# Aligning the programs of VectorE and ScalarE to blocks of 128 instructions in a fused LoRA matmul

## The chip, the cores and the metric

The kernel runs on one core of a Trainium2 chip. The metric is the device time of one execution in microseconds (us), the median of several runs. Before the change it is 161.82 us (three runs, 161.81 to 161.85).

## What is computed

A linear layer with a low-rank addition. `x` has 16 x 2048 = 32,768 rows of 256 numbers; the weights are 256 x 256, the rank is 16, and everything outside the kernel is float32.

```python
x_flat = x.reshape(-1, in_dim)
y = x_flat @ W
lora_out = x_flat @ lora_A
lora_out = lora_out * lora_E
lora_out = lora_out @ lora_B
y = y + scale * lora_out
return y.reshape(batch, seq_len, out_dim).astype(np.float32)
```

Some 33.6 MB have to be read and as many written.

## The kernel before

The kernel first folds the low-rank part into one matrix, `weff` = W + A diag(E) B, in bf16 (lines 159 to 177). After that the whole work is `x_flat @ weff`.

The rows are cut into five blocks of 56, 56, 48, 48 and 48 times 128 rows (`PLAN`). Three SBUF slots (`xy0` to `xy2`) hold a block each; x is loaded into a slot, the result is written over it in place, and the slot is stored from there. Block 3 uses slot 0 again and block 4 slot 1, so load 3 has to wait for store 0 and load 4 for store 1. Loads 0 to 3 are cut into pieces of 16 or 24 rows per partition (`PIECES`), each with its own semaphore; load 4 and all stores are single transfers. All of these are issued by SP (SyncE) in the order that the code writes out: loads 0 to 2, store 0, store 1, load 3, load 4, stores 2 to 4. Some have an extra wait: store 1 is issued after TensorE's 17th group of transposes, load 4 after the 19th, store 3 after the 28th (`ISSUE_STORE`, `ISSUE_LOAD`). lora_A, lora_B and lora_E are loaded from ScalarE's queue.

The computing goes in 32 steps of 8 x 128 rows. Per step `t`:

- VectorE casts 8 rows per partition to bf16 into `xb` (`rounded`, line 152), after a wait for the piece's load where a piece begins.
- TensorE transposes them into `psum_xt` (line 191), and VectorE copies that to `xt` (`copied`, line 156).
- TensorE multiplies with `weff` into `psum_y`, two halves of 4 x 128 rows (line 202).
- ScalarE copies each half back into the slot as float32 (line 225).

VectorE's order is `copied(t)`, `rounded(t + 2)`. VectorE's and ScalarE's programs are written out in full, all 32 steps; TensorE's is a loop of 16 rounds over two steps (line 212). At step 17 VectorE pauses (`HOLD = 17, 1`): it executes ten no-operations (lines 149 and 150) and then waits until store 1 has landed (line 151) before it casts step 17. All engines after VectorE pause with it.

The transfers written between lines 124 and 130 are issued before the meeting of all engines at line 132; the rest comes behind it. At the end VectorE, ScalarE, TensorE and SP count the semaphores back to zero (lines 245 to 253).

[...]

Of the kernel before, what the change touches and what calls it, by code (L numbers as in the profile page):

```python
# [35 lines left out]
def kernel(tc, x, W, lora_A, lora_B, lora_E, scale, out):  # L36
    nc = tc.nc
# [60 lines left out]
    def slot(i):  # L98
        return slots[i % LEAD][:, :PLAN[i], :]
# [20 lines left out]
        nc.tensor.wait_ge(sem, 1).then_inc(sem, -1)  # L120

    opening.append(tc.info.no_tile_sem_insts)
    transfer(nc.sync, s_w, out=w_sb, in_=W.rearrange("(p c) m -> p c m", c=KC))
# [17 lines left out]
    def rounded(t):  # L143
        i, r = steps[t]
        if (i, r) in s_ld:
            nc.vector.wait_ge(s_ld[i, r].sem, 16)
        if t == HOLD[0]:

            for _ in range(10):
                nc.vector.engine_nop()  # L150
            nc.vector.wait_ge(s_st[HOLD[1]].sem, 16)
        nc.vector.tensor_copy(out=xb[t % 2], in_=slot(i)[:, r:r + S, :]).then_inc(can_t[t % 2], 1)  # L152

# [22 lines left out]
    nc.vector.wait_ge(s_set.sem, 2)  # L176
    s_v.by(nc.vector.tensor_add(out=weff, in0=w_sb, in1=ps_aeb))  # L177
    rounded(0)
    rounded(1)
    for t in range(NS):  # L180
        copied(t)
        if t + 2 < NS:
            rounded(t + 2)
# [105 lines left out]
```

## Time and profile before

| what | value |
|---|---|
| median of three runs | 161.82 us (161.81 to 161.85) |
| the profiled execution's own time | 161.88 us |
| its span, first to last instruction | 160.6 us |
| moved by the DMA engines | 67.42 MB, mean 420 GB/s |
| busy: TensorE, VectorE, ScalarE | 93.9, 76.5, 63.2 us |
| granted TensorE clock, mean | 0.832 |

The span is shorter than the time by 1.3 us, which lies around it. Busy shares of the computing engines are between 39% and 58%, since they work in three stretches, with the pause from 55 to 87 us and the drain of the last stores, from 140 us, between and behind them. "DMA" in the chain of waits is time in which an instruction waited for a transfer to land. A bracket at the end of a timeline line gives the engine's idle time before that instruction and what ended it. In the list of DMA queues the columns are packets, MB, and the time that the packets took as a share of the span of all 16 DMA engines; asked for a window, the view counts the packets that start in it, so a share over 100% means only that they end outside it.

Beside the views, the trace holds every DMA packet with its start, duration and size, and every landing, 16 for each transfer (one of each DMA engine).

### The profile page before, as it was taken

The page shows a single profiled execution, that of the slowest core. Times are in us where ns is not written, and L with a number is a line of the kernel's source. Part 1 is how long each engine was busy: PE and PEld are TensorE (multiplying, and loading weights), DVE is VectorE, ACT ScalarE, POOL GpSimd, SP SyncE. Part 2 cuts the span into 40 slices and gives each one's busy share as a digit, 9 for nine tenths or more (in the row PEclk, how much of TensorE's full clock was granted, in tenths as well). Part 3 has the DMA queues.
Part 4 walks back from the last instruction along what each step waited for, and adds up shares of the span by engine and source line. Part 5 has one row for each costly group of instructions (what it writes and reads, how often), then busy time and mean ns, then how long its engine had stood idle before and what let it go on. Part 6 is the DMA issues. An engine that isn't in the chain of part 4 may idle for free.

```text
span 160.6 us, 1871 instructions
## 1 busy us (share of the span) xinstructions
PE 93.9 (58%) x780; PEld 84.2 (52%) x780; DVE 76.5 (48%) x67; ACT 63.2 (39%) x65; POOL 0.7 (0%) x6
## 2 busy tenths in 40 slices
PE   0159979999999920000000899999569999700000
PEld 0039959999999910000000789999458999500000
DVE  0178679998989300000002968987094985000000
ACT  1101746867777640000000077777605586800000
POOL 1000000000000000000000000000000000000000
PEclk9999999999999997555555599999955999995555
DMA  5999999999999999999998999999999999999994
GB/s 158 426 433 451 435 408 433 449 441 404 459 410 392 457 459 457 457 457 443 443 414 347 404 453 429 435 529 404 404 392 478 465 429 392 416 478 441 416 404 196
DMA packets 2658, 67.42 MB, mean 420 GB/s; under 512 B 464, under 2 KB 480, under 8 KB 608
## 3 DMA queue, kind: packets, MB, share of 16 engines
q1 hardware_dynamic: 2448, 67.37, 97.7%
q10 hardware_dynamic: 208, 0.03, 0.3%
q14 instruction: 2, 0.02, 0.0%
HBM read 33.85 MB, written 33.55 MB: 420 GB/s over the span
## 4 chain that ended last, share of the span: by engine, by line
PE 36%; DMA 34%; DVE 2%; ACT 1%; issue 0%; SPq 0%
PE psum_y L202 23%; DMA out_dram<-xy 20%; DMA xy<-in_x_dram 14%; PE psum_xt L191 13%; DVE xb L152 2%; ACT xy L225 1%; SPq L241 0%; SPq L236 0%
## 5 line engine op out<-in xcount | busy, mean ns | idle before, releaser
L225 ACT COPY xy<-psum_y 128x1024 f32<-128x1024 f32 x64 | 61.9, 1017 | 73.7 <-PE psum_y L202 73.7
L202 PE MATMUL psum_y<-weff,xt 128*128 128x256 bf16 x512 | 64.4, 281 | 0.1
L191 PE MATMUL psum_xt<-ident,xb 128*128 128x128 f32 x264 | 38.1, 293 | 37.9 <-DVE xb L152 37.9
L152 DVE CAST xb<-xy 128x2048 bf16<-128x2048 f32 x32 | 38.9, 1219 | 41.4 <-DMA out_dram<-xy 33.5
L202 PEld LDWEIGHTS psum_y<-weff,xt 128*128 128x128 bf16 x512 | 51.8, 101 | 7.4 <-issue 0.3
L191 PEld LDWEIGHTS psum_xt<-ident,xb 128*128 128x128 f32 x264 | 33.1, 152 | 39.6 <-DVE xb L152 39.2
L156 DVE COPY xt<-psum_xt 128x1024 f32<-128x1024 f32 x32 | 39.1, 1222 | 10.4 <-PE psum_xt L191 10.3
L164 PE MATMUL psum_xt<-ident,a_sb 128*16 128x128 f32 x2 | 0.6, 394 | 4.2 <-POOL ident L138 4.2
L160 DVE CAST b_bf<-b_sb 16x256 bf16<-16x256 f32 x1 | 0.3, 280 | 5.4 <-DMA b_sb<-in_lora_B_dram 5.4
L225 ACT ACT_TABLE_LOAD x1 | 1.3, 1283 | 3.5 <-PEq L132 3.5
L173 PE MATMUL psum_xt<-b_bf,ate 16*128 16x256 bf16 x2 | 0.6, 403 | 3.2 <-DVE ate L168 3.2
L164 PEld LDWEIGHTS psum_xt<-ident,a_sb 128*16 128x16 f32 x2 | 0.1, 90 | 4.2 <-DMA a_sb<-in_lora_A_dram 4.2
L173 PEld LDWEIGHTS psum_xt<-b_bf,ate 16*128 16x128 bf16 x2 | 0.1, 105 | 3.7 <-DVE ate L168 3.7
L168 DVE TENSOR_SCALAR ate<-psum_xt,e_sb 16x256 bf16<-16x256 f32 x1 | 0.5, 471 | 1.8 <-DMA e_sb<-in_lora_E_dram 1.8
L177 DVE TENSOR_TENSOR weff<-w_sb,psum_xt 128x512 bf16<-128x512 f32 x1 | 0.7, 689 | 0.8 <-PE psum_xt L173 0.8
L138 POOL TENSOR_SCALAR_AFFINE_SELECT ident<-ident 128x128 f32<-128x128 f32 x1 | 0.3, 293 | 0.2 <-POOL ident L136 0.2
L136 POOL MEMSET ident<- 128x128 f32 x1 | 0.2, 205 | 2.9 <-POOLq L132 2.9
L270 POOL MEMSET const-bfloat16-1.0<- 128x1 bf16 x1 | 0.1, 102 | 0.0
L270 POOL MEMSET const-uint8-127<- 128x1 uint8 x1 | 0.1, 102 | 0.0
L270 POOL MEMSET const-float32-0.0<- 128x1 f32 x1 | 0.1, 99 | 0.2 <-issue 0.2
L270 POOL MEMSET const-float32-1.0<- 128x1 f32 x1 | 0.1, 99 | 0.0
## 6 DMA issues: line engine op xcount, KB each, us to landing
xy<-in_x_dram SPq DMA_DIRECT2D x6, 3072.0 KB, 32.5
out_dram<-xy SPq DMA_DIRECT2D x3, 6144.0 KB, 21.5
out_dram<-xy SPq DMA_DIRECT2D x2, 7168.0 KB, 33.9
xy<-in_x_dram SPq DMA_DIRECT2D x4, 2048.0 KB, 17.6
xy<-in_x_dram SPq DMA_DIRECT2D x1, 6144.0 KB, 21.9
w_sb<-in_W_dram SPq DMA_DIRECT2D x1, 256.0 KB, 2.8
a_sb<-in_lora_A_dram ACTq DMA_DIRECT2D x1, 16.0 KB, 3.0
b_sb<-in_lora_B_dram ACTq DMA_DIRECT2D x1, 16.0 KB, 4.2
```

Source lines behind the costliest of these rows:

```text
L138: s_id.by(nc.gpsimd.affine_select(out=ident, in_=ident, compare_op=mybir.AluOpType.not_equal, fill=1.0, base=0, pattern=[[-1, P]], channel ...
L152: nc.vector.tensor_copy(out=xb[t % 2], in_=slot(i)[:, r:r + S, :]).then_inc(can_t[t % 2], 1)
L156: nc.vector.tensor_copy(out=xt[t % 2], in_=ps_xt[t % 2]).then_inc(can_m, 1)
L160: s_v.by(nc.vector.tensor_copy(out=b_bf, in_=b_sb))
L164: at_done = nc.tensor.transpose(ps_at[:, c, :], a_sb[:, c, :], ident)
L168: s_v.by(nc.vector.tensor_scalar(out=ate, in0=ps_at, scalar1=e_sb, scalar2=float(scale), op0=mybir.AluOpType.mult, op1=mybir.AluOpType.mult))
L173: aeb_done = nc.tensor.matmul(ps_aeb[:, c, :], ate[:, c, :], b_bf, start=True, stop=True)
L177: s_v.by(nc.vector.tensor_add(out=weff, in0=w_sb, in1=ps_aeb))
L191: done = nc.tensor.transpose(ps_xt[k][:, j, :], words[k][:, j, :], ident)
L202: done = nc.tensor.matmul(ps_y[h][:, j, :], pairs[k][:, h * G + j, :, c], weff[:, c, :], start=(c == 0), stop=(c == KC - 1))
L225: y = nc.scalar.copy(out=slot(i)[:, r:r + G, :], in_=ps_y[h])
L270: nc = _bacc.Bacc("TRN2", target_bir_lowering=False, num_devices=1)
```

## The change

Ahead of the first transfer, VectorE's and ScalarE's programs get an alignment directive. [...] The ten no-operations ahead of VectorE's wait in the pause are taken out. SP's, TensorE's and GpSimd's programs, every transfer, every wait and the order of all other instructions stay.

```diff
     def take(sem):
         nc.tensor.wait_ge(sem, 1).then_inc(sem, -1)
 
+
+    for engine in (nc.vector, nc.scalar):
+        engine.addr_align(128, offset=0, max_nops=0)
 
 
     opening.append(tc.info.no_tile_sem_insts)
@@ -145,9 +148,6 @@
         if t == HOLD[0]:
-
-            for _ in range(10):
-                nc.vector.engine_nop()
             nc.vector.wait_ge(s_st[HOLD[1]].sem, 16)
```

## The prediction

> **What bounds the kernel now.** I read the page first: the row of DMA busy tenths, the queues and the chain of waits; then the merged chain in order of time, the waits, the timeline around the places where VectorE waits, the DMA view of two short windows, and last the trace's single DMA packets.
>
> ```profile
> span 160.6 us, 1871 instructions
> DMA  5999999999999999999998999999999999999994
> q1 hardware_dynamic: 2448, 67.37, 97.7%
> q14 instruction: 2, 0.02, 0.0%
> ```
>
> The 16 DMA engines are busy in nearly every slice; the data queue alone fills 97.7% of their time. The last row is the code: two packets in the span, 0.02 MB together.
>
> ```profile
> 55.47 31.98 DMA out_dram<-xy
> ...
> 94.65 21.92 DMA xy<-in_x_dram
> ...
> 139.39 1.02 ACT xy L225
> ```
>
> ```profile
> DVE xb L152 <- DMA out_dram<-xy: 33.5, 1, 33.5
> DVE xb L152 <- DMA xy<-in_x_dram: 7.7, 2, 5.0
> ```
>
> ```profile
> 21.27 1.23 DVE L152 CAST xb<-xy 128x2048 bf16<-128x2048 f32 x1 [2.67 <-DMA xy<-in_x_dram]
> ```
>
> The computing engines wait for transfers: 2.67 us at the third piece of block 0, 33.46 us in the pause until store 1 has landed, 5.04 us for load 4. The chain's instructions end at 140.4 us; the remaining 20.2 us is the last store draining. The data queue takes transfers in order, and each is issued while others still run: store 1 at 55.47, while the data packets of store 0 run until about 69.1 to 70.0; load 4 at 94.65, with load 3 running until 100.6 to 101.6; store 3 at 124.55, store 2 running until 129.6 to 130.6; store 4 at 140.43, store 3 running until 144.1 to 145.6. No issue comes late, so the end is set by the work of the slowest DMA engine.
>
> That I take from the packet records. I sorted the data packets by start and strung each to the one that had just ended; 16 strings come out, one per DMA engine, each with 128 large packets of x and y, eight per 128-row transfer. A store packet of 57,344 bytes takes 2116 ns in the median, one of 49,152 bytes 1815. Thirteen engines put their last byte out at 158.61 to 159.20 us, and three later:
>
> - engine S at 159.47: it carried a code packet of 8,192 bytes at 108.02 (309 ns), and the data packet behind it took 2195 ns, 380 too many. Together 0.69.
> - engine V at 159.63: a code packet at 58.74 (309 ns), and 2474 ns for the next, 358 too many. Together 0.67.
> - engine Z at 160.06: no code packet. Its packets from 115.4 to 141.9, the stores during which TensorE and ScalarE compute, take 16 to 137 ns too long, about 1.10 us in all; during store 1, in the pause, they don't.
>
> Z's last landing, 160.54, ends the span.
>
> ```profile
> q1 hardware_dynamic: 80, 4.59, 106.1%
> q14 instruction: 1, 0.01, 0.2%
> issues: line engine op xcount, KB each, median us to landing
> out_dram<-xy SPq DMA_DIRECT2D x1, 7168.0 KB, 32.0
> ```
>
> That is the DMA view from 54 to 64 us: one code packet in the store phase. A second falls in the window from 104 to 112.
>
> **The change part by part.** *The ten no-operations* are recorded from 53.94 to 54.07 us: 0.13 us, inside the 33.46 us that VectorE waits anyway. Gain 0; without the pause 0.13.
>
> *Where the code packets go.* VectorE's no-operations run 4.7 us ahead of the packet at 58.74; ScalarE's copies at 102.7 to 103.3, about as many instructions into its program, run about 5 us ahead of the one at 108.02. I take these for the two engines that are aligned. That is inferred: the packets bear no engine's name. [...] After the alignment point VectorE has 99 instructions in the trace, 89 without the no-operations, and ScalarE 79; both fit in 128. [...]
>
> *What they cost there.* Before 1.75 us no data packet runs, and 15 of the engines have a gap of 0.10 to 0.96 us around 4 us between their first large packets (V 0.35, S 0.27). The trace doesn't show a code packet in the opening. Bounds: 0, if it falls into a gap, and 0.69 as in the middle. I take 0.3, nearer to the opening with its gaps. V then ends at 159.63 - 0.67 + 0.3 = 159.26 (158.96 to 159.65), S at 159.47 - 0.69 + 0.3 = 159.08 (158.78 to 159.47). Both stay ahead of Z even at the upper bound.
>
> *Z.* It carries neither packet. Its surplus goes with the computing during stores 2 and 3, which lasts as long as before: 24 us for 1.10 us, 0.05 per us. Z stays at 160.06, and with it the end.
>
> *What else moves.* V brings store 1's last landing (87.45; the next is 87.17) and load 4's (116.57; S 116.42, the next 116.15). Without these VectorE resumes 0.28 and 0.42 us earlier, and the last store is issued 0.42 earlier, behind 3.7 to 5.2 us of store 3. Gain 0; with that cover gone, up to 0.42. Shifting the computing by 0.42 us under Z's stores is 0.02.
>
> *The entry itself.* [...] Bounds: 0, and some 5 us as from the no-operations to the end of the code packet (54.0 to 59.05). ScalarE has the issues of lora_A, lora_B and lora_E behind it (0.74, 1.17, 1.65 us), and the meeting of all engines at L132, behind which SP issues the next five loads. SP's queue would not run dry: load 0 lands until 21.25 us. The set-up and the first steps would be late, up to 2.67 us of it swallowed at the third piece, the rest at the pause, since store 1 would go out at 58 instead of 55.5 and store 0 runs until 69.1. If that cover were gone, it would be one for one. I take 0.
>
> The sum: 0 for the no-operations, 0 for the packets on V and S as Z ends later, 0 at the entry, -0.02 to +0.02 on Z. The profiled execution took 161.88 (span 160.6 and 1.3 around it), its runs 161.82 in the median; the sum of 0 carries over, **161.8**.
>
> [...]
>
> **The rivals.**
>
> *Z is not there in the timed runs.* If Z's surplus comes from recording the computing (records written while stores are written), the timed runs end with V, and lose 159.63 less the slowest ordinary engine, 159.20 or V with its opening packet, 159.26: 0.37 to 0.43. That gives 161.4. For it: the surplus sits on one engine and only while instructions run during stores. Against it: the profiled execution took 161.88, only 0.06 above the median, where 0.4 would be expected.
>
> [...]
>
> *It does not do what it says.* The two packets belong to other engines, or a crossing remains late in the programs: V and S stay as they are, Z still ends, 161.8, not to be told from the forecast.
>
> **How the numbers follow.** A difference under 0.2%, 0.32 us, is about what a measurement of this kernel can't tell from no change. No change by Z, with the case that nothing moves: 0.43. Z absent, or smaller once V and S are out of its way: 0.35, at 161.4. Dearer front: 0.22, at 162.1 to 162.5. So faster 0.35, same 0.43, slower 0.22. The likeliest case's own range is 161.65 to 161.95. As both signs hold much of the chance, the range reaches to 161.3 (the full 0.43 and a tenth) and to 162.3, in the middle of the dearer front.
>
> **What would show it.** Right: no code packet between 20 us and the end, code packets in the first 5 us; V's and S's surplus of 0.67 and 0.69 gone, store 1's last landing near 87.2 and load 4's near 116.15, the pause and the wait for load 4 ending earlier, and still one engine without a code packet that ends some 0.9 us after the ordinary ones. Wrong on the entry: first issues of ScalarE later than 0.74 us, and lora_E landing after 7.45. Wrong on Z: all 16 engines ending within 0.6 us. The forecast falls if the last landing moves by more than 0.3 us, either way; if V or S ends last, the dearer front is the cause.

## The result, and the profile after

The kernel became slower. Sixteen runs of each beside one another: 162.65 us in the median (162.21 to 163.11) against 161.94 (161.81 to 162.82). The ratio over all runs is 1.0036, with a 95% interval of 1.0026 to 1.0047; the two medians alone lie 0.71 us apart, a ratio of 1.0044. The profiled execution of the changed kernel took 162.29 us with a span of 161.0; it is one of the three fastest of its sixteen, which has to be kept in mind when its trace is read. Every run has a span of its own, and the time lies 1.27 to 1.38 us above it in each run of the changed kernel.

The page of the changed kernel:

```profile
span 161.0 us, 1864 instructions
DMA  5999999999999999999988999999999999999994
q1 hardware_dynamic: 2448, 67.37, 98.0%
q14 instruction: 2, 0.02, 0.1%
```

The DMA engines are still busy in all slices, with the same packets and bytes, and there are still two code packets in the span, of 8,192 bytes each. They have moved. The DMA view of its first 6 us, and then that of 54 to 64 us, where one used to be:

```profile
q1 hardware_dynamic: 224, 1.57, 71.6%
q14 instruction: 2, 0.02, 1.5%
...
a_sb<-in_lora_A_dram ACTq DMA_DIRECT2D x1, 16.0 KB, 11.7
b_sb<-in_lora_B_dram ACTq DMA_DIRECT2D x1, 16.0 KB, 10.1
e_sb<-in_lora_E_dram ACTq DMA_DIRECT2D x1, 0.1 KB, 10.9
```

```profile
q1 hardware_dynamic: 78, 4.47, 103.5%
```

So far as forecast: both packets in the opening (at 1.79 us, 1102 ns long, and at 2.80, 309 ns), none later. Of the directive itself (line 124) the trace shows one branch on each engine, at 0.73 us on ScalarE (33 ns) and at 0.76 on VectorE (47 ns); this is the entry. The last column of the other lines was not: a small load now takes 10 to 12 us from issue to landing. The same loads in the kernel before:

```profile
a_sb<-in_lora_A_dram ACTq DMA_DIRECT2D x1, 16.0 KB, 3.0
...
e_sb<-in_lora_E_dram ACTq DMA_DIRECT2D x1, 0.1 KB, 5.8
```

The timeline of the kernel before (the issue of lora_A, the first cast, ScalarE's last copies ahead of the pause), then the timeline and the waits of the changed kernel:

```profile
0.74 0.40 ACTq L104 DMA_DIRECT2D a_sb<-in_lora_A_dram  x1
...
9.32 2.36 DVE L152 CAST xb<-xy 128x2048 bf16<-128x2048 f32 x2
...
56.28 1.93 ACT L225 COPY xy<-psum_y 128x1024 f32<-128x1024 f32 x2 [0.69 <-PE psum_y L202]
```

```profile
1.16 2.89 ACTq L104 DMA_DIRECT2D a_sb<-in_lora_A_dram  x1
1.17 6.91 SPq L104 DMA_DIRECT2D xy<-in_x_dram  x8
4.09 0.46 ACTq L104 DMA_DIRECT2D b_sb<-in_lora_B_dram  x1
4.57 0.44 ACTq L104 DMA_DIRECT2D e_sb<-in_lora_E_dram  x1
...
16.70 0.69 DVE L177 TENSOR_TENSOR weff<-w_sb,psum_xt 128x512 bf16<-128x512 f32 x1 [0.77 <-PE psum_xt L173]
17.31 2.35 DVE L152 CAST xb<-xy 128x2048 bf16<-128x2048 f32 x2
...
62.60 1.93 ACT L225 COPY xy<-psum_y 128x1024 f32<-128x1024 f32 x2 [0.69 <-PE psum_y L202]
```

```profile
DVE xb L152 <- DMA out_dram<-xy: 27.5, 1, 27.5
...
DVE xb L152 <- DMA xy<-in_x_dram: 4.8, 1, 4.8
```

The issue of lora_A takes 2.89 us instead of 0.40. By then SP has issued three pieces of x (from 1.17 to 3.01 us); the packets of the small loads run from 7.16 to 15.00 us instead of 2.11 to 7.10, lora_E lands at 15.4 us instead of 7.45, and the first cast starts at 17.31 instead of 9.32. The wait for block 0's third piece (2.67 us) is gone, swallowed, and VectorE's pause has shrunk from 33.5 to 27.5 us: the first stretch of computing ends at 64.5 us instead of 58.2 (the end of the last line of either timeline). That it is late costs the pause nothing; but for 6.3 us more it runs under store 0, which starts at about 52 us.

The chain of the changed kernel in order of time shows the same:

```profile
1.16 2.89 ACTq L104
4.57 10.87 DMA e_sb<-in_lora_E_dram
17.39 1.15 DVE xb L152
...
61.78 25.96 DMA out_dram<-xy
```

In the packet records, strung to DMA engines as in the prediction, thirteen engines end at 158.77 to 159.27 us (before: 158.61 to 159.20), two at 160.10 and 160.13, and one at 160.46. The last is the engine called Z before: its packets are too long in stores 2 and 3 again, by 1.08 us together, and now four of them under store 0 as well. The other two are late ahead of the first turn from loads to stores already: two engines land the first piece of load 2 some 0.34 us behind the others.

### The profile page after: what moved, and what is told of

Same layout as the page of the kernel before. It is cut to its first block, busy times and chain, and to the rows that moved or that the text cites. A ratio compares the mean times of both kernels' runs of the same rounds, so it can differ in the third digit from the quotient of the medians.

```text
span 161.0 us, 1864 instructions
## 1 busy us (share of the span) xinstructions
PE 92.3 (57%) x780; PEld 83.4 (52%) x780; DVE 76.5 (48%) x67; ACT 63.1 (39%) x65; POOL 0.7 (0%) x6
## 4 chain that ended last, share of the span: by engine, by line
PE 43%; DMA 36%; DVE 3%; ACTq 2%; ACT 1%; issue 1%; DVEq 0%; SPq 0%
PE psum_y L202 26%; PE psum_xt L191 17%; DMA out_dram<-xy 16%; DMA xy<-in_x_dram 13%; DMA e_sb<-in_lora_E_dram 7%; DVE xb L152 2%; ACTq L104 2%; ACT xy L225 1%; DVE weff L177 0%; PE psum_xt L173 0%; DVE ate L168 0%; ACTq L124 0%; DVEq L151 0%; DVEq L176 0%; SPq L241 0%
## 5 line engine op out<-in xcount | busy, mean ns | idle before, releaser
L202 PE MATMUL psum_y<-weff,xt 128*128 128x256 bf16 x512 | 63.5, 279 | 0.0
L152 DVE CAST xb<-xy 128x2048 bf16<-128x2048 f32 x32 | 38.9, 1217 | 32.3 <-DMA out_dram<-xy 27.5
L191 PEld LDWEIGHTS psum_xt<-ident,xb 128*128 128x128 f32 x264 | 32.6, 151 | 32.0 <-DVE xb L152 31.6
L156 DVE COPY xt<-psum_xt 128x1024 f32<-128x1024 f32 x32 | 39.1, 1223 | 10.5 <-PE psum_xt L191 10.5
```

Source lines behind the costliest of these rows:

```text
L156: nc.vector.tensor_copy(out=xt[t % 2], in_=ps_xt[t % 2]).then_inc(can_m, 1)
L191: done = nc.tensor.transpose(ps_xt[k][:, j, :], words[k][:, j, :], ident)
L202: done = nc.tensor.matmul(ps_y[h][:, j, :], pairs[k][:, h * G + j, :, c], weff[:, c, :], start=(c == 0), stop=(c == KC - 1))
```

## The experiments

Two theories. **Theory 1:** ScalarE's entry comes just ahead of its three loads; they go out late and queue behind x, the computing starts 8 us late, and more of it runs during store 0, where one DMA engine (Z) is slowed by it. **Theory 2**, the dearer front (a code packet costs more in the opening than in the middle) in another form: a code packet in the opening makes one DMA engine late, and each turn from loads to stores (the first around 51 us, the second around 115) charges the late engine again. Each kernel was run beside the kernel before.

| kernel | median us | before | ratio, 95% interval |
|---|---|---|---|
| e1 VectorE alone aligned | 162.16 | 162.02 | 1.0031 (1.0010 to 1.0051) |
| e2 ScalarE alone aligned | 162.38 | 162.02 | 1.0032 (1.0020 to 1.0045) |
| e4 ScalarE aligned behind its loads | 162.30 | 162.02 | 1.0022 (1.0004 to 1.0041) |
| e5 wait ahead of the loads | 161.95 | 162.02 | 0.9994 (0.9985 to 1.0003) |
| f1 loads issued behind the meeting | 162.31 | 161.89 | 1.0024 (1.0016 to 1.0033) |
| e3 no-operations gone alone | 161.89 | 161.89 | 0.9998 (0.9989 to 1.0007) |
| f3 two dummy rows | 161.92 | 161.89 | 1.0007 (0.9994 to 1.0021) |
| f5 aligned in the pause | 162.00 | 161.89 | 1.0009 (0.9997 to 1.0021) |
| f6 four dummy rows | 162.97 | 161.94 | 1.0057 (1.0043 to 1.0071) |
| f7 loads later still | 163.49 | 161.94 | 1.0103 (1.0088 to 1.0118) |
| f8 late loads and dummy rows | 162.34 | 161.93 | 1.0031 (1.0008 to 1.0053) |
| f9 third piece cut | 161.97 | 161.93 | 1.0000 (0.9982 to 1.0018) |

**VectorE alone**

```diff
-    for engine in (nc.vector, nc.scalar):
-        engine.addr_align(128, offset=0, max_nops=0)
+    nc.vector.addr_align(128, offset=0, max_nops=0)
```

> Only VectorE's program is aligned; ScalarE's stays where it was; the no-operations are gone. Theory 1 (ScalarE's entry holds back its three loads, which then queue behind x, so the computing starts 8 us late and runs on under store 0): lora_E lands near 7.5 us, the computing starts near 9.3, and the time is within 0.1 us of before. Theory 2 (code packets in the opening put one DMA engine late, which pays again at the turn from loads to stores): half of the loss stays, 0.2 to 0.4 us over before, with one code packet in the opening and one data engine that ends late.

Seven of twelve runs took 161.91 to 162.17 us, as before; five took 162.72 to 163.64. The small loads were on time (lora_A issued in 0.40 us at 0.74). So without theory 1's cause the common loss is gone, and what stays comes in some runs only: theory 2, but not as a shift of every run, as it was put, and larger than the 0.2 to 0.4 us. Such runs are rare without a packet in the opening: of all 120 runs of the kernel before, beside these kernels, three took more than 162.5 us, and f1, f5 and f9 below have one or two each.

**ScalarE alone**

```diff
+    nc.scalar.addr_align(128, offset=0, max_nops=0)
     opening.append(tc.info.no_tile_sem_insts)
```

> Only ScalarE's program is aligned, ahead of its three loads; VectorE keeps its place and its no-operations. Theory 1: the whole loss, 0.4 to 0.7 us over before; the issue of lora_A takes about 2.9 us instead of 0.4, lora_E lands near 15.8, weff near 17. Theory 2: half of it, 0.2 to 0.4 us.

Both at once: no run under 162.29, seven at 162.29 to 162.39, and five at 162.66 to 163.11. The median lies 0.36 above before, a little under theory 1's 0.4 to 0.7. The timeline of this kernel shows the cause of the common part:

```profile
1.16 2.87 ACTq L104 DMA_DIRECT2D a_sb<-in_lora_A_dram  x1
```

**ScalarE aligned behind its loads**

```diff
     transfer(nc.scalar, s_e, out=e_sb, in_=lora_E[:, None])
+    nc.scalar.addr_align(128, offset=0, max_nops=0)
```

> Both programs are aligned and the no-operations gone, but ScalarE's alignment stands behind its three loads. Theory 1: lora_E lands near 7.5 us, the computing starts before 11 us, and the time is that of before or up to 0.4 us less, with no code packet in the middle. Theory 2: two code packets still come in the opening, so 0.3 to 0.7 us over before.

VectorE's directive stays where the change put it. The loads are on time again (timeline and DMA view of the first 9 us of this kernel):

```profile
0.74 0.40 ACTq L104 DMA_DIRECT2D a_sb<-in_lora_A_dram  x1
```

```profile
q14 instruction: 2, 0.02, 0.4%
...
e_sb<-in_lora_E_dram ACTq DMA_DIRECT2D x1, 0.1 KB, 5.4
```

The floor is that of before: 161.89, and eight of twelve runs up to 162.49. Four took 163.05 to 163.31, which is theory 2. ScalarE's branch is recorded at 2.12 us and its next instruction at 2.55, while the code packets of this trace come only at 3.08 and 6.17, and the last one ahead of them ended 7.8 us before the span began: no code packet runs in these 0.43 us, so the entry of this trace does not wait for one.

**Late loads without alignment, first try**

```diff
+    nc.scalar.wait_ge(s_w.sem, 16)
     transfer(nc.scalar, s_a, out=a_sb, in_=lora_A.rearrange("(p c) r -> p c r", c=KC))
```

> The kernel before, with nothing aligned and the no-operations kept; ScalarE waits until W has landed (3.5 us) before it issues its three loads. Theory 1: the loss comes back without any alignment, 0.3 to 0.7 us over before; lora_E lands near 15, computing runs on to about 62 us under store 0. Theory 2: no change, since both code packets stay in the middle.

The edit missed: the three loads still went out at 0.74 to 1.65 us, and the wait came to stand behind them, at ScalarE's way into the meeting. It only held the meeting and with it SP's next five loads, by 0.85 us. So this run says nothing on theory 1; it shows that a meeting 0.85 us late is free (161.95 us against 162.02).

**Late loads without alignment**

```diff
-    transfer(nc.scalar, s_a, out=a_sb, in_=lora_A.rearrange("(p c) r -> p c r", c=KC))
-    transfer(nc.scalar, s_b, out=b_sb, in_=lora_B)
-    transfer(nc.scalar, s_e, out=e_sb, in_=lora_E[:, None])
...
     tc.compile()
+    transfer(nc.scalar, s_a, out=a_sb, in_=lora_A.rearrange("(p c) r -> p c r", c=KC))
+    transfer(nc.scalar, s_b, out=b_sb, in_=lora_B)
+    transfer(nc.scalar, s_e, out=e_sb, in_=lora_E[:, None])
```

> The kernel before, nothing aligned, the no-operations kept; ScalarE issues its three loads behind the meeting of all engines (about 3.3 us) instead of ahead of it (0.74), while both code packets stay in the middle. Theory 1 (late small loads, late computing, more computing under store 0): lora_E lands near 15 us, the first stretch of computing ends near 61, and all runs move up together by 0.3 to 0.5 us. Theory 2 (a code packet in the opening makes its DMA engine late, and the turns from loads to stores charge that engine again): no change.

The timeline of this kernel:

```profile
3.34 0.39 ACTq L104 DMA_DIRECT2D a_sb<-in_lora_A_dram  x1
...
13.79 0.28 DVE L160 CAST b_bf<-b_sb 16x256 bf16<-16x256 f32 x1 [13.79 <-DMA b_sb<-in_lora_B_dram]
...
62.37 1.93 ACT L225 COPY xy<-psum_y 128x1024 f32<-128x1024 f32 x2 [0.69 <-PE psum_y L202]
```

The loss is there with no alignment at all: ten of twelve runs lie between 162.15 and 162.44, together, 0.42 above before in the median (the other two took 162.57 and 164.72), and the last copy of the first stretch ends at 64.3 us, as in the changed kernel. Here Z ends at 160.53.

**The no-operations alone**

```diff
-            for _ in range(10):
-                nc.vector.engine_nop()
```

> Only the no-operations are taken out. VectorE's crossing then falls behind the pause, and its code packet comes at about 92 to 97 us, among loads 3 and 4 and ahead of the second turn (115 us), instead of at 58.7 under store 0. Theory 1: no change, within 0.1 us. Theory 2: its engine is late at the second turn; 0.1 to 0.7 us over before in some or all runs.

No change. VectorE's code packet moved from 58.7 to 91.7 us, and that shows that it is VectorE's and that the no-operations had set its place; the prediction had only inferred this. The DMA view of this kernel from 90 to 93 us:

```profile
q1 hardware_dynamic: 49, 1.20, 94.3%
q14 instruction: 1, 0.01, 0.6%
```

Theory 2 had expected a loss here, and it is not there in the times, though its trace has one packet at the second turn, at 114.4 us, 621 ns too long. In that trace the engine with this packet ends at 160.37 and Z at 159.94, and the run took 162.05, 0.16 over the median. So in this trace a packet between the turns is cheap: only one turn is left to charge it, and Z's own lateness covers most of what it charges there. That this holds in the other runs too was not shown.

**Dummy rows in the opening**

```diff
+    for k in range(2):
+        transfer(nc.scalar, s_d, out=dum[k:k + 1, :], in_=x_flat[8 * k:8 * k + 8, :].rearrange("(o r) k -> o (r k)", o=1))
     load(0)
```

`dum` is a buffer that nothing reads. f6 is the same with `range(4)`.

> The kernel before with two more transfers in the opening, each one row of 8 KB of x into a buffer that nothing reads, issued by ScalarE behind its three loads. No code is moved. Theory 2: if each row goes to one DMA engine, that engine is late at the first turn, and some runs are 0.8 to 1.1 us over before, as with the code packets. Theory 1: no change beyond the 0.6 us that a DMA engine needs for two rows, and no such runs. If the rows are spread over the 16 engines, the run says nothing on theory 2.

> As f3, with four rows of 8 KB instead of two. If they all go to one DMA engine, it is 4 x 0.31 = 1.2 us late at the first turn. Theory 2 (the turns charge the late engine again, 1.2 us at the first and 0.7 at the second as in the profiles of e2 and e4): most runs 0.5 to 2.3 us over before. Without a charge at the turns the engine would end at 158.9 + 1.2 = 160.1 us, no later than the last engine of before: no change.

The rows are single packets of 309 to 349 ns, like code. With two, eight of eleven runs stay at 161.72 to 162.05 and three take 162.31, 162.63 and 163.02; with four, all six are at 162.42 to 163.21. No code was moved, so in f6 a late DMA engine is enough; with two rows the interval of the ratio still holds 1. In f3's trace, of a high run (162.63), both rows lie on the string that ends last, at 160.93, with Z at 160.03. The landings show how the lateness grows. This is how far the last landing of a transfer lies behind the next one (for the changed kernel, whose last two are late, the third), in us, from the traces:

```
                                  before  changed    e2    e4    f3    f6
load 2, first piece  (45 us)        0.01     0.34  0.68  0.44  0.48  0.66
load 2, second piece (first turn)   0.08     0.67  1.42  1.07  1.00  1.34
load 4               (second turn)  0.15     0.61  1.59  1.76  1.15  1.63
last landing of store 4           160.54   160.94 161.50 161.69 161.25 161.65
```

In e2, e4, f3 and f6 an engine 0.4 to 0.7 us late on the loads leaves the first turn 1.0 to 1.4 us late, and the second 1.2 to 1.8. These four were profiled in runs of 162.63 to 163.07, high ones for e2, e4 and f3 and ordinary for f6. The traces of the changed kernel (162.29) and of e1 (161.92) come from low ones: e1's engine with the code packet is 0.32 us behind the next on the first row and 0.58 on the second, and ends at 160.02, just ahead of Z at 160.09; the last landing is at 160.57. So the growth to 1.2 us and more is shown for such runs only, and one trace of each kernel can't tell whether a lateness of 0.3 us is always let off. In the profiled execution of the kernel before no engine was late in the opening, and V and S got their packets behind the first turn.

**Alignment in the pause**

```diff
-            for _ in range(10):
-                nc.vector.engine_nop()
+            nc.vector.addr_align(128, offset=0, max_nops=0)
...
         n += 1
+        if n == 2 * HOLD[0] + 1:
+            nc.scalar.addr_align(128, offset=0, max_nops=0)
```

> Both programs are aligned, but VectorE's at the wait of the pause, in place of the no-operations, and ScalarE's ahead of step 17's first copy; both enter a new block while nothing is computed, and both code packets come at about 58 to 63 us, behind the first turn. Theory 1 and theory 2 both expect the time of before within 0.15 us, with no runs 0.8 us higher; were alignment itself, the branch or the entry dear, it would be slower by 0.3 us or more.

Eleven of twelve runs at 161.74 to 162.23, one at 162.87. Alignment and branch are not dear in themselves (0.11 us in the median here, 0.71 in the changed kernel); the place is. One detail missed: the code packets came at 56.9 and 97.3 us, the second much later than expected.

**A second dose of late computing**

```diff
     tc.compile()
+    nc.scalar.wait_ge(s_ld[0, 0].sem, 16)
     transfer(nc.scalar, s_a, out=a_sb, in_=lora_A.rearrange("(p c) r -> p c r", c=KC))
```

> As f1, but ScalarE issues its three loads only when the first piece of x has landed (9 us): a second dose of late computing with nothing else moved. Theory 1: lora_E lands near 20 us, the first stretch ends near 66 instead of 61, two or three more packets of one DMA engine are 0.1 us too long under store 0, and the time is 0.2 to 0.4 us over f1, 0.6 to 0.8 over before. If the loss of f1 came from something other than computing under store 0, f7 equals f1.

The dose is about right and the size isn't. The first stretch ended at 70.9 us, and the number of long packets under store 0 followed:

```
            first stretch ends   packets over 40 ns too long under store 0, on one engine
before            58.2 us        1, 118 ns
changed           64.5           4, 468 ns
f1                64.3           4, 472 ns
f7                70.9           7, 833 ns
```

(In before, f1 and f7 the strings follow this engine to the end and show it to be Z; in the changed kernel it is taken for Z by these. The packet right behind VectorE's code packet, where that falls under store 0, is on another engine and is not counted.) The kernels with one cause alone fit in: e1 and e4, with the loads on time, have one and two such packets, 104 and 165 ns, and e2, with late loads, has four, 482 ns.

That is theory 1's price: 0.35 us for the 6.1 to 6.3 us of the first dose, as much again for the 6.6 of the second. But f7 lost 1.55 us and not 0.6 to 0.8: all 16 engines ended at 160.09 or later, since at the turn from stores to loads, 83 to 90 us, and at the second turn, 113 to 116 us, packets of all engines were too long (13.9 and 10.5 us together, 1.1 at either place in f1). Why the turns became dear for all of them was not found.

**Both causes without alignment**

> Nothing aligned: the three loads issued behind the meeting as in f1, and the two dummy rows in the opening as in f3. If the loss of the changed kernel is the sum of these two, this looks like it: no run under 162.1 us, a part of the runs 0.3 to 0.9 higher, a median of 162.3 to 162.8. If alignment itself adds something, this stays below the changed kernel by 0.2 us or more.

The edit is f1's and f3's together. No run is under 162.21; nine lie at 162.21 to 162.46, the others at 162.82, 163.05 and 164.19. The floor of the changed kernel (162.21) is reproduced; its median, 0.31 higher, is not. By the sign named above, 0.2 us or more below the changed kernel, something of it is missing here: more of its runs are high (13 of 16 over 162.4, against five of twelve). And f8's trace, of a high run (163.05), is not plain theory 2. Strung to engines, both rows lie on one engine; it is charged 1.07 us at the first turn, nothing at the second, and ends at 160.39. The last to end, at 161.22, has the too-long packets under stores 2 and 3, so it is Z, which starts store 2 at 116.62 there and at 115.93 in f1. Why Z is late there was not found.

**A version meant to beat both**

```diff
-PIECES = {0: [16, 16, 24],
+PIECES = {0: [16, 16, 8, 16],
```

> A version meant to beat both: nothing aligned, no no-operations, and block 0's third piece cut into 8 and 16 rows, so that VectorE does not wait 2.7 us for it at 18.6 us. Theory 1: the first stretch ends near 53.7 us instead of 56.3, one or two packets of the slow DMA engine under store 0 lose their 0.1 us; 0.05 to 0.2 us below before. Theory 2 and others: no change.

No change. The wait for the third piece fell from 2.67 to 0.48 us, but VectorE then waited 2.11 us for another piece at 38.3 us; the last copy of the first stretch ended only 1.3 us earlier (56.9 against 58.2), and 1.3 us are worth 0.07 at theory 1's price. No version was found that is faster than the kernel before; e3 equals it without the ten no-operations.

## Why the prediction was wrong

The forecast was 161.8, no change, with 161.3 to 162.3 as its range; measured were 162.65. The step that failed is the entry, taken at 0 with what lies behind it; the packets in the opening were mis-sized besides. By its steps:

- *The no-operations, 0*: right. e3 alone measures 0.9998.
- *Both code packets leave the middle and come in the opening, and they belong to VectorE and ScalarE*: right, shown by the DMA view, by e1, e2 and e3. That programs of 89 and 79 instructions need no packet in the middle since they fit in 128 was the author's reading, and no run tests the 128. What the runs show is the places: 58.7 and 108.0 us before, 1.79 and 2.80 in the changed kernel, 91.7 for VectorE's with the no-operations gone (e3), 56.9 and 97.3 with the alignment in the pause (f5).
- *The entry, "I take 0"*: this is the step that failed first, and it moves every run. The entry itself is short, 0.43 us from the branch to the next instruction in e4, but ScalarE's first issue behind it took 2.9 us. The bound of 5 us covered that issue; it did not cover what came next, the small loads queuing behind x, which made 2.9 us into 8.0 at the first cast. The prediction read lora_E's 5.8 us to landing, with its issue at 1.65 us, as a given; issued behind more of x it took 10.9 (at 4.57, changed kernel) and 12.3 (at 9.43, f7).
- *What lies behind the entry*: the prediction let the lateness beyond 2.67 us end at the pause, at no cost, since store 0 still ran. The same text gave a price for it, 0.05 us on Z for each us of computing during stores, and used it only for stores 2 and 3. 6.3 us of it under store 0 make 0.3; Z ended 0.40 later (160.46 against 160.06) and f1 measures 0.42 on the time. The mechanism was in hand, and the term was left out of the sum.
- *The packets in the opening, 0.3 each, bounds 0 and 0.69*: mis-sized. Two engines of the changed kernel end at 160.10 and 160.13, 0.8 to 0.9 after the slowest ordinary one, where 159.26 and 159.08 were forecast. The lateness of 0.34 us is not the cost; the turns add to it. In this execution, a low one, both are still ahead of Z, as the prediction had it. In e2 and e4 that engine ends 0.9 to 1.2 us after Z.
- *The dearer front*, at 162.1 to 162.5, was the nearest rival. It reckoned with two code packets for each aligned engine; no run shows that, e1 and e2 have one for the one engine that they align. One is enough where the turns add to it (e2): an ordinary engine has to lose 1.10 us to end behind Z (160.06 less 158.96), and in e2, e4, f3 and f6 the turns at 51 and 115 us reach that from 0.4 to 0.7.
- *Z absent from the timed runs*: nothing speaks for it. The time rose where this rival had it fall, and one engine's packets under stores 2 and 3 are 0.97 to 1.12 us too long in every trace. What Z does in an execution that is not recorded is not shown.
- *VectorE resumes 0.28 and 0.42 us earlier*: wrong sign. Store 1 and load 4 landed 0.3 to 0.4 us later than before (87.75 and 116.94), because two late engines now brought them. That a shift of this size costs nothing was forecast, and it was not measured by itself.

So two things make the changed kernel slower: a shift of all runs by about 0.4 us (Z under store 0, shown by e2 and f1, and absent in e1 and e4), and in many runs up to 0.9 more, which came with a code packet in the opening (e1, e2, e4), or four dummy rows without one (f6), and only in single runs of f1. That a DMA engine made late is what costs this 0.9 is shown by the traces of e2, e4, f3 and f6, where the engine that was late on the loads ends last; none of e1's high runs was traced. Whether the two together make up the whole loss is not shown, since f8 falls short by 0.31 in the median. With one code packet in the opening, 5 of 12 runs (e1) and 5 of 12 (e2) were high; if two packets on two engines bring their chances independently, 1 - (7/12)(7/12) = 66% of the runs of the changed kernel should be. Of its sixteen runs 13 are over 162.4, the top of the low group of e2. That would also leave f8, with both rows on one engine, lower. But e4 speaks against it: it has two code packets in the opening as well, and only five of its twelve runs are over 162.4. So the share of high runs in the changed kernel is not explained. Why an issue right behind ScalarE's entry takes 2.9 us, and why a late engine is charged in some runs only, stay open.

## What to carry to other kernels

Where DMA engines never rest (98.0% busy with data here), ask of each code or helper transfer not only how long it is but which engine it makes late, and whether a turn between loads and stores is still ahead; behind the first turn the same packet was nearly free here (ratios of 0.9998 in e3 and 1.0009 in f5). Keep small loads that a whole stretch of work needs ahead of the large ones in issue order: 2.6 to 2.9 us of delay behind the first x pieces made 8 us at the consumer. And computing that is hidden in time can still cost by what it runs under (some 0.35 us for 6.3 us under store 0): use a price found for one stage in every stage that the change moves work into.

## What the runs showed that was not expected

- The issue of lora_A takes 2.87 to 2.89 us just behind ScalarE's entry (changed kernel, e2), and 0.38 to 0.42 elsewhere. SP's third issue of x, at the same time, took 0.85 to 0.90 instead of 0.43.
- An 8 KB packet on one of 16 busy DMA engines, 0.31 us by itself, seems able to cost the kernel 0.7 to 1.6 us (e1's five high runs, over 162.02) when it comes ahead of the first turn from loads to stores; those five runs were not traced.
- The turn itself: packets of x from 48.5 to 53 us are together 4.3 us too long in the kernel before and 10.6 in the changed one, over all 16 engines. That sum does not follow the late engine: it is 6.3 to 9.5 in e3, e5, f1, f5 and f9, which have none in the opening, and 4.3 in f6, which has one. The longest single packet does so better: 1.2 to 1.3 us too long in e2 and e4 and 0.86 in f6, against 0.48 to 0.71 in the kernel before and those five.
- One DMA engine writes its 49,152 bytes too slowly, by up to 0.14 us of 1.8 in the kernel before and 1.1 us over 16 packets, while the computing engines run; in the pause, from 71 to 84 us, every packet of 57,344 bytes takes 2.12 us, whatever the engine. Why was not found.
